# One encoder layer on one core: new orders of loads and output tiles, and weight sums made by accumulating loads instead of by GpSimd

## The chip, the cores and the metric

The kernel runs on one core of a Trainium2 chip: a tensor engine (TensorE, PE, with PEld loading its weights), a vector engine (VectorE, DVE), a scalar engine (ScalarE, ACT), GpSimd (POOL) and SyncE (SP), which only issues DMAs here. The metric is device time in microseconds (us) of one launch. Three runs of the kernel before took 1179.47, 1179.75 and 1180.17 us, median 1179.75.

## The reference

One layer of a streaming encoder on 1024 tokens of width 1024, in float32:

```
hn = rmsnorm(h)                       z = hn @ w_in
u, q, k, v = split(z)
h += concat(pool_mixer(u), chunk_attention(q, k, v)) @ w_out
hn = rmsnorm(h)                       up = hn @ w_up           # 1024 x 5632
gt, val = up[..., :2816], up[..., 2816:]
h += (gelu(causal_dwconv(gt)) * val) @ w_down
hn = rmsnorm(h)
h += sigmoid(hn @ w_ple_gate + b) * (p @ w_ple)
out = rmsnorm(h)
```

## The kernel before

Activations lie transposed, features on the partitions and tokens along the free axis, in two halves of 512 tokens (`HS[0]`, `HS[1]`). Every float32 product is three matmuls of split operands, `mm3` (lines 118 to 120: high by high, high by low, low by high). `split` makes the two parts: ACT copies the high part (line 123), DVE subtracts to get the low one (line 124).

**Start.** x arrives as 16 loads `x[k, h]`; beside them come parts of `w_qk0` (buffer `wq`) and of `w_v`. ACT makes the high part of the scaled x (line 215), DVE the low part (line 216), both are split parts of matmul operands. After each k, `start_mm(k)` adds the k-th terms: 12 matmuls 512 wide for q and k, and 9 matmuls 256 wide for the first three tiles of V.

**Attention, output projection.** Attention and pooling follow, then the output projection `out_mm` for the first half of the tokens and then, one output tile of 128 features after another, for the second. Around the second half the operands of the next stage ("forms") are made with `put`, a `split` into form n at place j.

**Up-projection.** Each of the 22 feature tiles `fi` holds gate and value columns. A 2 x 2 block product of weights (quarters 11, 12, 21, 22: gate or value by the first or second half of the input features) and activations (`b11, b12, b21, b22`) is done with seven products instead of eight, in the order 1, 5, 2, 6, 3, 7, 4, each 12 matmuls 512 wide. Products 1, 2 and 4 take a quarter of `w_up` as it is; 5, 6, 3 and 7 take sums or differences of quarters. A list `order` holds all products; `prepare` runs three ahead of the product being computed: it issues loads (`fetch`, SP), forms the sum (`summed`, line 687, a POOL operation on 128 x 512) in one of five raw buffers `rawu`, and splits it into one of three weight buffers `wu`. So the split for a product can start when the product three places earlier has left its buffer. Scheduling is by program order on each engine, with `high_priority` moving these splits and `keep` ahead of other work.

`step` takes what a product leaves in PSUM: `keep` (line 765) copies a result to SBUF on ACT; its copies of product 1 (`np1`) and 5 are used later; `u2` (line 781) is DVE's sum of product 6 with `np1`; lines 783 to 793 combine the rest; `gate` (802 to 805) is convolution and GELU; `values_in` (808, 809) multiplies the branches. Even tiles have 16 down-projection tiles of the pair of tiles before them placed after products 6, 3, 7 and 4; odd tiles have none, nor do tiles 0, 1, 20 and 21. Tile 0's products 1, 2, 5 and tile 1's product 1 come ahead of the rest, so that tile 0 goes on with 6, 3, 7, 4 after 5.

The last down-projections, the embedding gate and the final norm end the kernel.

Of the kernel before, what the change touches and what calls it, by code (L numbers as in the profile page):

```python
# [83 lines left out]
def trunk(tc, xT, pT, vecs, w_qk0, w_in, w_v, bias, counts, pool_w, w_out, w_up, w_down,  # L84
# [4 lines left out]
    with tc.tile_pool(name="sb", bufs=1) as sb, \  # L89
# [32 lines left out]
        def split(src, hi, lo):  # L122
            act.activation(hi, src, AF.Copy)  # L123
            dve.tensor_tensor(lo, src, rv(hi), ALU.subtract)  # L124
# [62 lines left out]
            return PS[:, (4, 5, 6, 4, 5, 6, 7, 3)[t], 0:256]  # L187

        def start_mm(k):
            for c in range(2):  # L190
                for h in range(2):
                    mm3(PS[:, 2 * c + h], w0h[:, k, c * P:(c + 1) * P], w0l[:, k, c * P:(c + 1) * P],
                        XTH[h][:, k], XTL[h][:, k], k == 0, k == KT - 1)
            for t in range(VT0):
                v_mm(t, k, v_ps(t), wv1)

# [6 lines left out]
        for k in range(KT):  # L203
            xs = xraw[k]
            for h in range(2):
                sp.dma_start(xs[:, h * 512:(h + 1) * 512], xT[k, :, h * 512:(h + 1) * 512])
                if k == 0 and h == 0:
                    act.dma_start(vec, vecs)
                if k in (0, 1, 4) and h == 0:
                    ke = (1, 4, 0, 0, 8)[k]  # L210
                    sp.dma_start(wq[:, k:ke], w_qk0[:, k * 256:ke * 256].rearrange("p (k c) -> p k c", c=256))
            g = vec[:, C_GMIX + k:C_GMIX + k + 1]
            for h in range(2):
                xk = xs[:, h * 512:(h + 1) * 512]
                act.activation(XTH[h][:, k], xk, AF.Copy, scale=g)
                dve.scalar_tensor_tensor(XTL[h][:, k], xk, g, rv(XTH[h][:, k]), ALU.mult, ALU.subtract)  # L216
                if h == 0:
                    split(wq[:, k], w0h[:, k], w0l[:, k])
            if k % 2 == 0:
                wv = wvraw[k // 2]  # L220
                sp.dma_start(wv, w_v[0, :, k * 256:(k + 2) * 256])
                wv = wv.rearrange("p (k c) -> p k c", k=2)
                split(wv, wv1[0][:, k:k + 2], wv1[1][:, k:k + 2])
# [10 lines left out]
        start_mm(KT - 1)  # L234

        def v_out(t, half, ps):
            s = rstd_tok[:, t:t + 1]
# [404 lines left out]
        def form_at(kb):  # L642
            a = r(kb, 4096).rearrange("p (x k t) -> p x k t", x=2, k=4)
            return a[:, 0], a[:, 1]

        forms = {1: form_at(64), 2: form_at(48), 3: form_at(16), 4: form_at(80), 5: form_at(0),
                 6: form_at(96), 7: form_at(112)}

        def put(n, j, src):
            split(src, forms[n][0][:, j], forms[n][1][:, j])  # L650


        wu = [r(32 + 4 * s, 1024).rearrange("p (x k c) -> p x k c", x=2, k=4) for s in range(3)]
# [1 line left out]
        rawd = f(42, 512)  # L655
        rst = f(44, SEQ)
        ahead = [(0, 1), (1, 1), (0, 2), (0, 5)]
        alone = ahead[:3]
        steps = {0: (6, 3, 7, 4), 1: (5, 2, 6, 3, 7, 4)}
        for fi in range(2, NF):  # L660
            steps[fi] = (1, 5, 2, 6, 3, 7, 4)
        order = ahead + [(fi, n) for fi in range(NF) for n in steps[fi]]

        loads = []
        for i, (fi, n) in enumerate(order):
            if (fi, n) in alone:
                loads += [(i, (fi, n), q) for q in FORMS[n]]
            else:
                need = {1: ((0, 0),), 5: ((1, 0), (1, 1)), 2: ((0, 1),), 6: ((0, 0),), 3: ((0, 1),), 7: (), 4: ()}[n]
                loads += [(i, fi, q) for q in need if not any(l[1] == fi and l[2] == q for l in loads)]  # L670
        prepared, fetched, done = [0], [0], [0]
        held = {}
        used = [False] * len(rawu)

        def fetch(upto):

            while fetched[0] < len(loads) and loads[fetched[0]][0] < upto and not used[fetched[0] % len(rawu)]:
                _, owner, (v, z) = loads[fetched[0]]
                i = fetched[0] % len(rawu)
                fetched[0] += 1  # L680
                used[i] = True
                fi = owner if isinstance(owner, int) else owner[0]
                sp.dma_start(rawu[i], w_up[fi, v, :, z * 512:(z + 1) * 512])
                held[owner, (v, z)] = i

        def summed(to, a, b, op=ALU.add):
            pool.tensor_tensor(rawu[to], rawu[a], rawu[b], op)  # L687
# [1 line left out]
        def prepare(upto):  # L689
            while prepared[0] < min(upto, len(order)):  # L690
                fi, n = order[prepared[0]]
                w_ = wu[prepared[0] % 3]
                prepared[0] += 1
                fetch(prepared[0] + 2)
                assert fetched[0] == len(loads) or loads[fetched[0]][0] >= prepared[0]
                if (fi, n) in alone:
                    t, = done_with = [held[(fi, n), q] for q in FORMS[n]]
                else:
                    a11, a12, a21, a22 = [held.get((fi, q)) for q in ((0, 0), (0, 1), (1, 0), (1, 1))]
                    if n == 5:  # L700
                        summed(a21, a21, a22)
                    elif n == 6:
                        summed(a21, a21, a11)
                    elif n == 3:
                        summed(a11, a21, a12)
                    elif n == 7:
                        summed(a21, a21, a22, ALU.subtract)
                    t = {1: a11, 5: a21, 2: a12, 6: a21, 3: a11, 7: a21, 4: a22}[n]
                    done_with = {3: [a11, a12], 7: [a21], 4: [a22]}.get(n, [])
                with tc.high_priority(AHEAD):  # L710
                    split(rawu[t].rearrange("p (k c) -> p k c", k=4), w_[:, 0], w_[:, 1])
                for q in done_with:
                    used[q] = False

        def product(bank, first):

            i = done[0]
            prepare(i + 1)
            fh, fl = forms[order[i][1]]
            w_ = wu[i % 3]  # L720
            for k in range(4):
                mm3(PS[:, bank], w_[:, 0, k], w_[:, 1, k], fh[:, k], fl[:, k], first and k == 0, k == 3, not first)
            done[0] += 1
            prepare(i + 4)

# [7 lines left out]
            weighted(0, d)  # L733
        for k in range(4):
            put(1, k, b11[k])
        for d in range(KT):
            out_mm(d, 1, d % 6, range(8), True, True)
            dve.tensor_tensor(H[d][:, HS[1]], H[d][:, HS[1]], PS[:, d % 6], ALU.add)
            norm_b.add(d)
            weighted(1, d)  # L740
            if d == 0:
                norm_a.sums()
            if d == 1:
                norm_a.rows(rst[:, HS[0]])
            if d < 4:
                pool.tensor_tensor(part[d % 2], b11[d], b12[d], ALU.subtract)
                put(5, d, part[d % 2])
# [76 lines left out]
        for n, src in ((7, b12), (4, b21)):  # L824
            for k in range(4):
                put(n, k, src[k])
# [4 lines left out]
        wd = [(B[:, 4096:5120], B[:, 5120:6144]), (B[:, 6144:7168], r(44, 1024))]  # L831

        def down_weights(fi, dst, raws=(rawd,)):
            for z in range(2):
# [63 lines left out]
        wg = [r(b, 2048) for b in (48, 56, 96, 104, 16, 24, 80, 88)]  # L898
        hp = [[(r(b, 512), r(b + 2, 512)) for b in bs]
              for bs in ((112, 116, 120, 124, 32, 36, 40, 44), (0, 4, 8, 12, 64, 68, 72, 76))]  # L900
        rawg = [f(44, 1024), f(48, 1024), f(52.25, 1024)]
        ng = [0]

# [168 lines left out]
```

## Time and profile before

| | |
|---|---|
| median of three runs | 1179.75 us (1179.47 to 1180.17) |
| the profiled execution's own time | 1180.88 us |
| its span, first to last instruction | 1179.1 us |
| granted TensorE clock, mean | 0.996 |
| instructions | 15388 |
| DMA | 70.79 MB in 34777 packets, mean 60 GB/s |

The profile's first part gives each engine's busy time with its share of the span in brackets and the number of its instructions after an x. In a group, "line engine operation out<-in xcount" is followed by the busy time, the mean of one in ns and the idle time ahead of it with what ended most of that. A row of the timeline begins with start and duration in us; a bracket at its end is the idle time ahead of it and what released it. A row of the waits names who waited, for whom, us in total, how often, and the longest. A row of windows gives the busy time of PE, PEld, DVE, ACT and POOL with counts, then the granted clock, the DMA share and GB/s. A row of the DMA issues gives the tensor, the queue, the count, the size of one and the median time from issue to landing.

### The profile page before, as it was taken

How to read it: one execution, taken by the hardware profiler on the slowest of the kernel's cores; microseconds unless marked ns; L12 is line 12 of the kernel's file. 1: busy time of each engine (PE TensorE's matmuls, PEld its weight loads, DVE VectorE, ACT ScalarE, POOL GpSimd, SP SyncE). 2: the span in 40 equal slices, each digit the busy share in tenths (PEclk: the TensorE clock that was granted, in tenths of full speed). 3: DMA queues.
4: the chain of work that ended last, by engine and by line, in shares of the span. 5: the costliest groups of instructions: out<-in, count | busy, mean ns of one | idle time of the engine just before them, and what ended most of it. 6: DMA issues, size and time to landing. Idle time of an engine off the chain costs nothing.

```text
span 1179.1 us, 15388 instructions
## 1 busy us (share of the span) xinstructions
PE 1159.2 (98%) x5829; PEld 979.5 (83%) x5829; DVE 876.2 (74%) x1405; ACT 542.1 (46%) x932; POOL 217.9 (18%) x194
## 2 busy tenths in 40 slices
PE   9999999999999989999999999999999999999996
PEld 7988998888888778888888888888888887888896
DVE  7678877879457887868777777777777779894454
ACT  7568686765555433324242424142424244554333
POOL 0000000181012431212121212121212123141000
PEclk9999999999999999999999999999999999999998
DMA  7110101106300120202020212111112121500021
GB/s 257 37 48 30 48 14 64 48 20 196 116 27 1 57 87 27 81 28 80 24 75 28 72 37 70 38 63 45 63 37 71 36 71 46 185 29 1 12 73 60
DMA packets 34777, 70.79 MB, mean 60 GB/s; under 512 B 3984, under 2 KB 6288, under 8 KB 34704
## 3 DMA queue, kind: packets, MB, share of 16 engines
q1 hardware_dynamic: 34560, 69.75, 18.2%
q8 instruction: 45, 0.74, 0.3%
q14 instruction: 28, 0.23, 0.1%
q10 hardware_dynamic: 144, 0.07, 0.0%
HBM read 65.61 MB, written 4.19 MB: 59 GB/s over the span
## 4 chain that ended last, share of the span: by engine, by line
PE 59%; issue 3%; DVE 2%; DMA 1%; POOL 1%; ACT 0%; DVEq 0%; POOLq 0%; ACTq 0%
PE PS L119 20%; PE PS L118 20%; PE PS L120 20%; DVE R L124 1%; POOL F L687 1%; DMA F<-in_w_down 1%; DMA F<-in_w_up 0%; DVE V L788 0%; DVE F L809 0%; PE PS L602 0%; ACT R L123 0%; DVE F L793 0%; PE PS L610 0%; DVE F L781 0%; DVE V L808 0%
## 5 line engine op out<-in xcount | busy, mean ns | idle before, releaser
L118 PE MATMUL PS<-R 128*128 128x512 f32 (+1 forms) x1144 | 430.0, 376 | 7.0 <-DVE F L781 3.2
L120 PE MATMUL PS<-R 128*128 128x512 f32 (+1 forms) x1144 | 426.7, 373 | 0.0
L119 PE MATMUL PS<-R 128*128 128x512 f32 (+1 forms) x1080 | 408.4, 378 | 0.3 <-DVE R L216 0.3
L118 PEld LDWEIGHTS PS<-R 128*128 128x128 f32 x1144 | 215.5, 188 | 45.0 <-ACT F L765 2.3
L120 PEld LDWEIGHTS PS<-R 128*128 128x128 f32 x1144 | 215.6, 188 | 38.2 <-DVE R L124 0.2
L123 ACT ACTIVATE R<-F 128x512 fp32r<-128x512 f32 (+2 forms) x217 | 135.3, 638 | 217.7 <-PE PS L119 173.0
L119 PEld LDWEIGHTS PS<-R 128*128 128x128 f32 x1080 | 203.6, 188 | 36.9 <-DVE R L216 0.9
L687 POOL TENSOR_TENSOR F<-F 128x512 f32<-128x512 f32 x88 | 139.4, 1584 | 512.2 <-DVE R L124 374.0
L124 DVE TENSOR_TENSOR R<-F,R 128x512 fp32r<-128x512 f32 (+2 forms) x213 | 161.1, 764 | 22.0 <-ACT R L123 19.3
L119 PE MATMUL PS<-B 128*128 128x512 f32 (+1 forms) x376 | 144.8, 385 | 0.0
L118 PE MATMUL PS<-B 128*128 128x512 f32 (+1 forms) x376 | 144.2, 383 | 0.0
L847 DVE TENSOR_TENSOR F<-F,PS 128x512 f32<-128x512 f32 x160 | 107.3, 683 | 21.6 <-PE PS L120 21.4
L123 ACT ACTIVATE B<-F 128x512 fp32r<-128x512 f32 (+1 forms) x83 | 58.0, 722 | 110.4 <-PE PS L119 74.4
L118 PEld LDWEIGHTS PS<-B 128*128 128x128 f32 x376 | 70.7, 188 | 15.0
L119 PEld LDWEIGHTS PS<-B 128*128 128x128 f32 x376 | 70.6, 188 | 14.3
L120 PE MATMUL PS<-B,R 128*128 128x512 f32 (+1 forms) x224 | 81.1, 362 | 0.0
L120 PE MATMUL PS<-B 128*128 128x512 f32 (+1 forms) x216 | 81.0, 375 | 0.0
L124 DVE TENSOR_TENSOR B<-F,B 128x512 fp32r<-128x512 f32 (+1 forms) x63 | 51.3, 841 | 9.6 <-ACT B L123 9.4
L338 ACT ACTIVATE F<-F,small 128x640 f32<-128x640 f32 (+2 forms) x64 | 44.4, 694 | 21.2 <-DVE small L336 13.0
L594 ACT ACTIVATE F<-F 128x512 f32<-128x512 f32 (+1 forms) x49 | 27.9, 570 | 51.2 <-DVE F L972 24.3
L360 DVE TENSOR_TENSOR B<-PS,B 128x640 fp32r<-128x640 f32 (+2 forms) x64 | 42.0, 656 | 9.2 <-ACT B L359 8.2
L120 PEld LDWEIGHTS PS<-B 128*128 128x128 f32 x216 | 40.5, 188 | 8.3
(145 smaller groups left out, 1560.2 us busy)
## 6 DMA issues: line engine op xcount, KB each, us to landing
F<-in_w_up SPq DMA_DIRECT2D x91, 256.0 KB, 2.6
F<-in_w_down SPq DMA_DIRECT2D x44, 256.0 KB, 2.6
F<-in_w_in SPq DMA_DIRECT2D x10, 512.0 KB, 3.5
F<-in_xT SPq DMA_DIRECT2D x16, 256.0 KB, 6.1
F<-in_w_out SPq DMA_DIRECT2D x16, 256.0 KB, 2.8
F<-in_xT SPq DMA_DIRECT2D x8, 512.0 KB, 3.6
F<-in_w_gate SPq DMA_DIRECT2D x8, 512.0 KB, 3.5
F<-in_bias SPq DMA_DIRECT2D x8, 320.0 KB, 2.9
```

The source lines that it names most:

```text
L118: pe.matmul(ps, ahi, bhi, start=first, stop=False, skip_group_check=more)
L119: pe.matmul(ps, ahi, blo, start=False, stop=False, skip_group_check=more)
L120: pe.matmul(ps, alo, bhi, start=False, stop=last, skip_group_check=more)
L123: act.activation(hi, src, AF.Copy)
L124: dve.tensor_tensor(lo, src, rv(hi), ALU.subtract)
L338: act.activation(S[:, 0:n], S[:, 0:n], AF.Exp, bias=s_[:, 0:1], scale=-1.0, accum_out=s_[:, 1:2])
L360: dve.tensor_tensor(lo, pst, rv(hi), ALU.subtract)
L594: act.activation(self.q, src, AF.Square)
L687: pool.tensor_tensor(rawu[to], rawu[a], rawu[b], op)
L847: dve.tensor_tensor(H[d][:, HS[h]], H[d][:, HS[h]], PS[:, bank], ALU.add)
```

## The change

Four parts, in one edit.

1. *Sums by accumulating loads.* For tiles in `by_load`, here all 22, `fetch` loads the first quarter of a chain with SP and issues the others as accumulating DMAs from POOL's queue into the same buffer. Product 5's buffer later grows into 6 (after the split for 5) and 3 (after the split for 6) by two further accumulating loads issued in `prepare`; 7's is a buffer of its own. Each tile then takes five loads on SP and four accumulating ones on POOL. `fetch` runs one place earlier for these tiles.

```
+        by_load = range(NF)
+        chains = {1: ((0, 0),), 5: ((1, 0), (1, 1)), 2: ((0, 1),), 7: ((1, 0), (0, 0)), 4: ((1, 1),)}
+        grows = {5: (0, 0), 6: (0, 1)}
...
+                if place >= upto + (fi in by_load):
+                    break
...
+                sp.dma_start(rawu[i], quarter(fi, qs[0]))
+                for q in qs[1:]:
+                    pool.dma_start(rawu[i], quarter(fi, q), accum_op=ALU.add)
...
-                if (fi, n) in alone:
-                    t, = done_with = [held[(fi, n), q] for q in FORMS[n]]
+                if fi in by_load:
+                    m = n if n in chains else 5
+                    t = held[(fi, m), chains[m][0]]
+                    done_with = [] if n in grows else [t]
...
                     split(rawu[t].rearrange("p (k c) -> p k c", k=4), w_[:, 0], w_[:, 1])
+                if fi in by_load and n in grows:
+                    pool.dma_start(rawu[t], quarter(fi, grows[n]), accum_op=ALU.add)
```

2. *Start.* The matmuls of `start_mm` run half by half, the V matmuls of step k run after the q and k matmuls of step k+1 (`start_v(k - 1)`), `w_v` is loaded in odd steps, and the parts of `w_qk0` at other places.

```
-                if k in (0, 1, 4) and h == 0:
-                    ke = (1, 4, 0, 0, 8)[k]
+                if (k, h) in ((0, 0), (0, 1), (3, 1)):
+                    ka, ke = {(0, 0): (0, 1), (0, 1): (1, 4), (3, 1): (4, 8)}[k, h]
...
+                if k % 2 and h == 0:
+                    sp.dma_start(wvraw[k // 2], w_v[0, :, (k - 1) * 256:(k + 1) * 256])
...
             if k < KT - 1:
                 start_mm(k)
+            if k:
+                start_v(k - 1)
```

3. *Output tiles of the second half* in the order 0, 4, 1, 5, 2, 6, 3, 7; the puts of forms 6 and 7 are made among them, those of form 2 and POOL's subtractions on b21 are spread. Forms lie at other addresses.

```
-        for d in range(KT):
-            out_mm(d, 1, d % 6, range(8), True, True)
+        for z, d in enumerate((0, 4, 1, 5, 2, 6, 3, 7)):
+            k = z // 2
+            out_mm(d, 1, z % 6, range(8), True, True)
...
-                k = d - 4
-                put(2, k, b21[k])
                 dve.tensor_tensor(b12[k], b12[k], b22[k], ALU.subtract)
                 dve.tensor_tensor(b11[k], b11[k], b12[k], ALU.subtract)
-                pool.tensor_tensor(b21[k], b21[k], b11[k], ALU.subtract)
-            if d == 5:
+                put(6, k, b11[k])
+                put(7, k, b12[k])
+            for j in {2: (0,), 4: (1, 2), 6: (3,)}.get(z, ()):
+                put(2, j, b21[j])
+            for j in {2: (0,), 4: (1,), 5: (2,), 7: (3,)}.get(z, ()):
+                pool.tensor_tensor(b21[j], b21[j], b11[j], ALU.subtract)
+            if z == 5:
                 prepare(3)
...
-        for k in range(4):
-            put(6, k, b11[k])
         step(0, 2)
```

4. *Last tile.* The `w_down` tiles of the last two feature tiles are loaded and split one after product 3, one after product 4, instead of both after 3.

```
-                             3: lambda: [down_weights(fi, wd2[fi % 2], raw_last[fi % 2]) for fi in last_f]})
+                             3: lambda: down_weights(last_f[0], wd2[0], raw_last[0]),
+                             4: lambda: down_weights(last_f[1], wd2[1], raw_last[1])})
```

How instructions stand on an engine, at three places. A row is line, operation, output<-input, size, and the semaphores waited for; PE, Activation, DVE and Pool are those of engines, DMAHW those of loads issued by SP, DMASW those of loads issued by POOL.

ACT at the start, from the first x tile on, before. Line 215 makes the high part of x, line 224 is the square, the row into `B` is the split of `w_v`:

```order
L215 ACTIVATE R<-F,vec 128x512 [waits DMAHW1_49,DMAHW0_49]
L123 ACTIVATE R<-F 128x256 [waits DMAHW2_49]
L215 ACTIVATE R<-F,vec 128x512 [waits DMAHW3_49]
L123 ACTIVATE B<-F 128x512 [waits DMAHW4_49]
L224 ACTIVATE F<-F 128x1024 [waits DVE_49]
L215 ACTIVATE R<-F,vec 128x512 [waits DMAHW5_49]
L123 ACTIVATE R<-F 128x256 [waits DMAHW6_49]
L123 ACTIVATE R<-F 128x256
L215 ACTIVATE R<-F,vec 128x512 [waits DMAHW7_49]
```

The same place after the change, where line 219 is x and line 226 the square:

```order
L219 ACTIVATE R<-F,vec 128x512 [waits DMAHW1_49,DMAHW0_49]
L123 ACTIVATE R<-F 128x256 [waits DMAHW2_49]
L219 ACTIVATE R<-F,vec 128x512 [waits DMAHW3_49]
L123 ACTIVATE R<-F 128x256 [waits DMAHW4_49]
L226 ACTIVATE F<-F 128x1024 [waits DVE_49]
L219 ACTIVATE R<-F,vec 128x512 [waits DMAHW5_49]
L123 ACTIVATE B<-F 128x512 [waits DMAHW6_49]
L219 ACTIVATE R<-F,vec 128x512 [waits DMAHW7_49]
L123 ACTIVATE R<-F 128x256
```

The split of `w_v` moved behind the second x tile, and a split of `w_qk0` stands ahead of the square.

ACT in an even tile, from the split for product 5 on, before. Line 805 is GELU, line 765 the copy of product 1 (`np1`); the splits that wait for Pool are those for 5, 6 and 3:

```order
L123 ACTIVATE R<-F 128x512 [waits PE_49,Activation_49,Pool_49]
L123 ACTIVATE R<-F 128x512 [waits DMAHW6_49,PE_49,Activation_49]
L805 ACTIVATE F<-F 128x1024 [waits DVE_49]
L123 ACTIVATE R<-F 128x512 [waits PE_49,Pool_49]
L765 ACTIVATE F<-PS 128x512 [waits PE_49]
L123 ACTIVATE R<-F 128x512 [waits PE_49,Activation_49,Pool_49]
```

After the change, GELU is line 827 and the copy is line 787, the splits for 5 and 6 wait for DMASW:

```order
L123 ACTIVATE R<-F 128x512 [waits DMASW0_49,PE_49,Activation_49]
L123 ACTIVATE R<-F 128x512 [waits DMAHW1_49,PE_49,Activation_49]
L827 ACTIVATE F<-F 128x1024 [waits DVE_49]
L123 ACTIVATE R<-F 128x512 [waits DMASW2_49,PE_49,Activation_49]
L787 ACTIVATE F<-PS 128x512 [waits PE_49]
L123 ACTIVATE B_3423<-F 128x512 [waits DVE_49,Activation_49]
L787 ACTIVATE V<-PS 128x512 [waits PE_49]
L123 ACTIVATE B_3423<-F 128x512 [waits DVE_49]
```

The split ahead of the copy of `np1` now waits for an accumulating load instead of a POOL operation, and a split for the down-projection (into `B`) stands between the two copies, where that for product 3 stood.

DVE in the last tile, from the value product (line 809) to u2 (line 781), before; 793 is `gate0`:

```order
L809 TENSOR_TENSOR F<-F,V 128x1024 [waits DVE_49]
L124 TENSOR_TENSOR R<-F,R 128x512 [waits PE_49,Activation_49]
L124 TENSOR_TENSOR R<-F,R 128x512 [waits DMAHW7_49]
L124 TENSOR_TENSOR R<-F,R 128x512 [waits DMAHW5_49]
L124 TENSOR_TENSOR R<-F,R 128x1024 [waits DVE_49,Activation_49]
L124 TENSOR_TENSOR R<-F,R 128x512 [waits PE_49,Activation_49]
L793 TENSOR_TENSOR F<-PS,F 128x512
L124 TENSOR_TENSOR R<-F,R 128x512 [waits DMAHW4_49,Activation_49]
L124 TENSOR_TENSOR R<-F,R 128x512 [waits DMAHW3_49]
L781 TENSOR_TENSOR F<-PS,F 128x512 [waits PE_49]
```

After the change, with u2 on line 803, `gate0` on 815 and the value product on 831:

```order
L831 TENSOR_TENSOR F<-F,V 128x1024 [waits DVE_49]
L124 TENSOR_TENSOR R<-F,R 128x512 [waits DMAHW5_49,PE_49,Activation_49]
L124 TENSOR_TENSOR R<-F,R 128x512 [waits DMAHW6_49,Activation_49]
L124 TENSOR_TENSOR R<-F,R 128x1024 [waits DVE_49,Activation_49]
L124 TENSOR_TENSOR R<-F,R 128x512 [waits DMASW7_49,PE_49,Activation_49]
L124 TENSOR_TENSOR R<-F,R 128x512 [waits DMASW5_49,PE_49,Activation_49]
L815 TENSOR_TENSOR F<-PS,F 128x512
L803 TENSOR_TENSOR F<-PS,F 128x512 [waits PE_49]
```

Two subtractions of the `w_down` splits fewer stand ahead of u2, and the two weight splits ahead of `gate0` wait for accumulating loads.

More of the change, by code (lines that the diff above doesn't have):

```diff
@@ L189, in start_mm, with start_v @@
         def start_mm(k):
-            for c in range(2):
-                for h in range(2):
+            for h in range(2):
+                for c in range(2):
                     mm3(PS[:, 2 * c + h], w0h[:, k, c * P:(c + 1) * P], w0l[:, k, c * P:(c + 1) * P],
                         XTH[h][:, k], XTL[h][:, k], k == 0, k == KT - 1)
+        def start_v(k):
             for t in range(VT0):
@@ L218, in trunk @@
                     split(wq[:, k], w0h[:, k], w0l[:, k])
[L219 to L223, printed above, removed]
+            if k % 2:
+                wv = wvraw[k // 2].rearrange("p (k c) -> p k c", k=2)
+                split(wv, wv1[0][:, k - 1:k + 1], wv1[1][:, k - 1:k + 1])
             act.activation(xs, xs, AF.Square)
@@ L234, in trunk @@
         start_mm(KT - 1)
+        start_v(KT - 1)
         def v_out(t, half, ps):
@@ L640, in trunk @@
                for n in (range(2, 10), (10, 11, 12, 13, 14, 15, 0, 1))[h]] for h in range(2)]
[L642 to L647, printed above, removed]
+        form_kb = {1: (64, 68, 72, 76), 2: (44, 48, 52, 56), 3: (16, 20, 24, 28), 4: (80, 84, 88, 92),
+                   5: (0, 4, 8, 12), 6: (96, 104, 112, 120), 7: (100, 108, 116, 124)}
+        forms = {n: [(r(kb, 512), r(kb + 2, 512)) for kb in kbs] for n, kbs in form_kb.items()}
         def put(n, j, src):
-            split(src, forms[n][0][:, j], forms[n][1][:, j])
+            split(src, *forms[n][j])
         wu = [r(32 + 4 * s, 1024).rearrange("p (x k c) -> p x k c", x=2, k=4) for s in range(3)]
@@ L657, in trunk @@
         ahead = [(0, 1), (1, 1), (0, 2), (0, 5)]
-        alone = ahead[:3]
         steps = {0: (6, 3, 7, 4), 1: (5, 2, 6, 3, 7, 4)}
@@ L662, in trunk @@
         order = ahead + [(fi, n) for fi in range(NF) for n in steps[fi]]
+        by_load = range(NF)
+        chains = {1: ((0, 0),), 5: ((1, 0), (1, 1)), 2: ((0, 1),), 7: ((1, 0), (0, 0)), 4: ((1, 1),)}
+        grows = {5: (0, 0), 6: (0, 1)}
         loads = []
         for i, (fi, n) in enumerate(order):
-            if (fi, n) in alone:
-                loads += [(i, (fi, n), q) for q in FORMS[n]]
+            if fi in by_load:
+                if n in chains:
+                    loads.append((i, (fi, n), chains[n]))
             else:
                 need = {1: ((0, 0),), 5: ((1, 0), (1, 1)), 2: ((0, 1),), 6: ((0, 0),), 3: ((0, 1),), 7: (), 4: ()}[n]
-                loads += [(i, fi, q) for q in need if not any(l[1] == fi and l[2] == q for l in loads)]
+                loads += [(i, fi, (q,)) for q in need if not any(l[1:] == (fi, (q,)) for l in loads)]
         prepared, fetched, done = [0], [0], [0]
@@ L675, in fetch @@
         def fetch(upto):
-            while fetched[0] < len(loads) and loads[fetched[0]][0] < upto and not used[fetched[0] % len(rawu)]:
-                _, owner, (v, z) = loads[fetched[0]]
+            while fetched[0] < len(loads) and not used[fetched[0] % len(rawu)]:
+                place, owner, qs = loads[fetched[0]]
+                fi = owner if isinstance(owner, int) else owner[0]
+                if place >= upto + (fi in by_load):
+                    break
                 i = fetched[0] % len(rawu)
@@ L681, in fetch, with quarter @@
                 used[i] = True
-                fi = owner if isinstance(owner, int) else owner[0]
-                sp.dma_start(rawu[i], w_up[fi, v, :, z * 512:(z + 1) * 512])
-                held[owner, (v, z)] = i
+                sp.dma_start(rawu[i], quarter(fi, qs[0]))
+                for q in qs[1:]:
+                    pool.dma_start(rawu[i], quarter(fi, q), accum_op=ALU.add)
+                held[owner, qs[0]] = i
+        def quarter(fi, q):
+            return w_up[fi, q[0], :, q[1] * 512:(q[1] + 1) * 512]
         def summed(to, a, b, op=ALU.add):
@@ L695, in prepare @@
                 assert fetched[0] == len(loads) or loads[fetched[0]][0] >= prepared[0]
-                if (fi, n) in alone:
-                    t, = done_with = [held[(fi, n), q] for q in FORMS[n]]
+                if fi in by_load:
+                    m = n if n in chains else 5
+                    t = held[(fi, m), chains[m][0]]
+                    done_with = [] if n in grows else [t]
                 else:
@@ L718, in product @@
             prepare(i + 1)
-            fh, fl = forms[order[i][1]]
+            form = forms[order[i][1]]
             w_ = wu[i % 3]
             for k in range(4):
-                mm3(PS[:, bank], w_[:, 0, k], w_[:, 1, k], fh[:, k], fl[:, k], first and k == 0, k == 3, not first)
+                mm3(PS[:, bank], w_[:, 0, k], w_[:, 1, k], *form[k], first and k == 0, k == 3, not first)
             done[0] += 1
@@ L823, in trunk @@
         norm_b.rows(rst[:, HS[1]])
-        for n, src in ((7, b12), (4, b21)):
-            for k in range(4):
-                put(n, k, src[k])
+        for k in range(4):
+            put(4, k, b21[k])
         t_pool.__exit__(None, None, None)
@@ L830, in trunk @@
         gv = [B[:, 2048 * s:2048 * (s + 1)] for s in range(2)]
-        wd = [(B[:, 4096:5120], B[:, 5120:6144]), (B[:, 6144:7168], r(44, 1024))]
+        wd = [(B[:, 4096:5120], B[:, 5120:6144]), (B[:, 6144:7168], r(60, 1024))]
         def down_weights(fi, dst, raws=(rawd,)):
```

16 lines of the change are left out of this document (8 added, 8 removed).

## The prediction

> **What bounds the kernel now.** I read the page first, then TensorE's busy time in windows, then the waits of TensorE, and last the timeline around each wait.
>
> ```profile
> PE 1159.2 (98%) x5829; PEld 979.5 (83%) x5829; DVE 876.2 (74%) x1405; ACT 542.1 (46%) x932; POOL 217.9 (18%) x194
> 480.00:520.00 40.00, 40.00 (x176) 32.80 (x175) 31.46 (x42) 12.84 (x18) 9.76 (x6) 1.00 0.10 34
> ```
>
> The second row is 40 us of the up-projection: TensorE is busy all of it at a granted clock of 1.00, 176 matmuls, so one starts every 40/176 = 0.227 us and a product of 12 lasts 2.73 us. The change removes no matmul. POOL's 9.76 us and a DMA share of 0.10 are cover, not bound. Time can only come from the few places where TensorE stops; of its waits these three concern the change:
>
> ```profile
> PE PS L118 <- DVE F L781: 3.2, 2, 1.7
> PE PS L118 <- ACT F L765: 1.9, 1, 1.9
> PE PS L118 <- ACT V L765: 0.9, 1, 0.9
> ...
> 394.64 0.50 PE L118 MATMUL PS<-R 128*128 128x512 f32 x1 [0.86 <-ACT V L765]
> 415.47 0.47 PE L118 MATMUL PS<-R 128*128 128x512 f32 x1 [1.43 <-DVE F L781]
> 428.53 0.50 PE L118 MATMUL PS<-R 128*128 128x512 f32 x1 [1.92 <-ACT F L765]
> 1001.14 0.47 PE L118 MATMUL PS<-R 128*128 128x512 f32 x1 [1.73 <-DVE F L781]
> ```
>
> Call the four stops A, B, C, D: 0.9 + 1.4 + 1.9 + 1.7 = 5.9 us, all at the entry to the up-projection or just after its last tile. That is the most the change can give there. Everywhere else in the 22 tiles a sum has hidden cover, and the question is whether what replaces it has cover too.
>
> **The price of an accumulating load.** The change drops 88 sums on POOL and issues 88 accumulating loads from POOL's queue; w_up transfers go from 91 to 198 (110 on SP, 88 on POOL).
>
> ```profile
> L687 POOL TENSOR_TENSOR F<-F 128x512 f32<-128x512 f32 x88 | 139.4, 1584 | 512.2 <-DVE R L124 374.0
> F<-in_w_up SPq DMA_DIRECT2D x91, 256.0 KB, 2.6
> F<-in_w_in SPq DMA_DIRECT2D x10, 512.0 KB, 3.5
> F<-in_xT SPq DMA_DIRECT2D x16, 256.0 KB, 6.1
> 394.34 0.33 SPq L836 DMA_DIRECT2D F<-in_w_down  x1
> ```
>
> This trace has no accumulating load and no DMA of POOL's at all. Let L be the time from POOL being released to the sum standing in the buffer. Low bound: a plain load of the same 256 KB, 2.6. High bound: the same load while eight queue at the start, 6.1. I take 4.1: 2.6, plus 0.9 for 256 KB more on the way (3.5 - 2.6; the destination is read as well as written), plus 0.6 for POOL's part of the issue, the middle between nothing and what one POOL pass over the tile takes beyond SP's issue (1.58 - 0.33 = 1.25). It is nearest to the 512 KB row, since 16 engines at a share of 0.10 are not the crowd of the 6.1 row. The 107 additional transfers of 256 KB are 28 MB over some 620 us, 45 GB/s on top of 34: a cost of nothing while the share stays near 0.2.
>
> The Trainium skill, "DMA: Bandwidth & Descriptors", section "Anatomy of one DMA — SWDGE (gpsimd) path", gives a load issued by GpSimd 2.0 us plus bytes over 436 GB/s, an estimate of 2.6 for one without addition; by it L would sit at my low bound and the sum below would be 0.5 lower. No run so far shows it.
>
> An addition cannot start before the buffer's split is done (wake 0.1, an estimate), and a split after it takes 0.63 on ACT, then DVE 0.69: 1.3.
>
> **A, entry to tile 0 (saves 0.6).** ACT's copy `keep` stands behind puts that wait for POOL's subtractions on b21, queued behind POOL's sums. Those sums go and the puts are spread. New: tile 0 runs 5, 6, 3 consecutively, so two additions are in series into one buffer.
>
> ```profile
> 382.40 0.69 DVE L124 TENSOR_TENSOR R<-F,R 128x512 fp32r<-128x512 f32 x1
> ```
>
> Split 5 ends at 383.1; two rounds of 0.1 + L + 1.3 end at 385.9 + 2L = 394.1 for L = 4.1. TensorE could go on at 394.64 - 0.86 = 393.8. Left over 0.3, saved 0.6; 2 us for each us of L.
>
> **B (saves 1.4).** DVE is behind by 1.4 us when u2 (L781) is due. Operations beside a POOL sum were stretched:
>
> ```profile
> 398.19 1.78 DVE L124 TENSOR_TENSOR R<-F,R 128x512 fp32r<-128x512 f32 x1
> 403.09 2.29 DVE L803 SCALAR_TENSOR_TENSOR F<-F,vec 128x1024 f32<-128x1024 f32 x1 [0.72 <-ACT F L802]
> ...
> 542.06 1.28 DVE L803 SCALAR_TENSOR_TENSOR F<-F,vec 128x1024 f32<-128x1024 f32 x1
> ```
>
> L124 takes 1.78 against 0.69, L803 2.29 against 1.28 away from POOL: 2.1 us back from these two alone, and the puts of forms 6 and 7 leave this stretch for the output projection. Both exceed 1.4. What is next there is another POOL-free operation, so I give all 1.4.
>
> **C (saves 1.9).** The copy of np1 stood on ACT behind the split of a w_down load, with a second split between:
>
> ```profile
> 426.85 0.63 ACT L123 ACTIVATE B<-F 128x512 fp32r<-128x512 f32 x1 [0.41 <-DMA F<-in_w_down]
> 427.90 0.58 ACT L765 ACTIVATE F<-PS 128x512 f32<-128x512 f32 x1
> ```
>
> The new order on ACT puts split 6 and `keep` ahead of the w_down split. If split 6 is on time, the stop goes: 1.9.
>
> **D, last tiles (saves 1.5).** u2 stood behind seven splits on DVE, five of them in the last row but one below; two of the seven, of a w_down tile, move one product later.
>
> ```profile
> 965.87 0.69 DVE L124 TENSOR_TENSOR R<-F,R 128x512 fp32r<-128x512 f32 x1
> 977.47 0.39 PE L118 MATMUL PS<-R 128*128 128x512 f32 x1
> 984.94 0.69 DVE L124 TENSOR_TENSOR R<-F,R 128x512 fp32r<-128x512 f32 x1
> 996.53 0.39 PE L118 MATMUL PS<-R 128*128 128x512 f32 x1
> 994.58 4.02 DVE L124 TENSOR_TENSOR R<-F,R 128x512 fp32r<-128x512 f32 x5 [0.62 <-ACT R L123]
> 1000.32 0.68 DVE L781 TENSOR_TENSOR F<-PS,F 128x512 f32<-128x512 f32 x1
> ```
>
> Two splits fewer are 2 x 0.69 = 1.4 and their waits, so the 1.7 goes. But tiles 20 and 21 have no down-projection between products: from split 5 (ends 966.6 and 985.6) two rounds end at 969.4 + 2L and 988.4 + 2L, and product 3 is due at 977.5 and 996.5. Both need L up to 4.05; at 4.1 they are late by 0.1 each. Saved 1.7 - 0.2 = 1.5, slope 4 for each us of L.
>
> **Steady tiles (0).** Ten even tiles, 2 to 20. Their rows:
>
> ```profile
> 543.25 0.69 DVE L124 TENSOR_TENSOR R<-F,R 128x512 fp32r<-128x512 f32 x1
> 544.02 3.99 POOL L687 TENSOR_TENSOR F<-F 128x512 f32<-128x512 f32 x2 [5.35 <-DVE R L124]
> 546.73 0.63 ACT L123 ACTIVATE R<-F 128x512 fp32r<-128x512 f32 x1 [0.49 <-PE PS L119]
> 547.27 0.58 ACT L765 ACTIVATE F<-PS 128x512 f32<-128x512 f32 x1
> 549.42 0.39 PE L118 MATMUL PS<-R 128*128 128x512 f32 x1
> ```
>
> Split 5 ends at 543.94. ACT's split 6 now waits for the addition and stands ahead of the copy of np1, which product 2 (549.42) needs. So 543.94 + 0.1 + L + 0.63 + 0.58 must not pass 549.42: L up to 4.2. At 4.1 it fits by 0.1 us; beyond 4.2 it costs 10 us for each us of L. Odd tiles:
>
> ```profile
> 528.35 0.69 DVE L124 TENSOR_TENSOR R<-F,R 128x512 fp32r<-128x512 f32 x1 [0.73 <-ACT R L123]
> 535.82 0.39 PE L118 MATMUL PS<-R 128*128 128x512 f32 x1
> ```
>
> Split 6 ends at 529.04 and product 3 starts at 535.82: 529.04 + 0.1 + L + 1.3 fits for L up to 5.4, another 10 us for each us beyond. POOL's queue is in order: the additions for 5 and 7 are ahead of those for 6 and 3 and wait only for loads, issued a product earlier than before. Behind a late one stands the next POOL addition and no one else.
>
> **Start (+0.8).** V matmuls move a step later, w_v loads move behind x, and ACT no longer splits w_v before the first square.
>
> ```profile
> 4.00:8.00 4.00, 2.89 (x8) 1.53 (x7) 2.09 (x5) 1.74 (x3) 0.00 (x0) 1.00 0.82 213
> 8.00:12.00 4.00, 3.77 (x11) 3.00 (x12) 1.51 (x3) 2.87 (x6) 0.00 (x0) 0.57 1.04 399
> 12.00:16.00 4.00, 4.00 (x25) 3.49 (x24) 4.00 (x8) 4.00 (x7) 0.00 (x0) 1.00 0.97 346
> 7.44 0.50 PE L118 MATMUL PS<-R 128*128 128x512 f32 x1 [1.06 <-ACT R L215]
> 12.70 0.74 DVE L216 SCALAR_TENSOR_TENSOR R<-F,vec,R 128x512 fp32r<-128x512 f32 x1
> ```
>
> By data both orders are tied to the x tile whose low half L216 finishes at 13.4: TensorE holds the same matmuls by then. But without V matmuls in the first step it can run dry at 10.5 to 11.4, and here a gap of 1.06 us was followed by four microseconds at 0.57 of the clock. A second such window loses 4 x 0.43 = 1.7. I take half, 0.8 (bounds: -1, the gap of 1.06 filled; +1.7).
>
> The Trainium skill, "TensorE: Matmul & The Clock Gate", section "Why this matters for your kernels", asks only that TensorE not idle over about 3 us; by it no window is lost and the sum is 0.8 lower. The trace disagrees so far: 0.57 after a gap of 1.06.
>
> **Sum.** -0.6 - 1.4 - 1.9 - 1.5 + 0.8 = -4.6 us. The profiled execution took 1180.88 us, so 1176.3; the median shown, 1179.75, is 1.1 below that execution, so the forecast is **1175.2 us**. For other L the change is -4.6 + 6(L - 4.1), with 10(L - 4.2) added above 4.2: -2.4 at 4.3, 0 at 4.45, +8.8 at 5.0, +12 at 5.2.
>
> **The rivals.**
>
> *The copy of np1 comes late in every even tile (slower).* For: 0.1 us of slack, on an L that no row shows, and ACT's order puts `keep` behind the addition. Against: low bound 2.6 leaves 1.6 of slack. It decides from L = 4.45; with L = 5.0 the time is 1179.75 + 8.8 = 1188.6, and with 5.2 1191.8.
>
> *POOL is held up by DVE while it issues (slower).* For: POOL and DVE stretch each other in this trace:
>
> ```profile
> 546.77 1.78 DVE L788 TENSOR_TENSOR V<-V 128x512 f32<-128x512 f32 x1
> ```
>
> One DVE operation of 1.28 to 1.78 ahead of each issue makes L 5.4 to 5.9: +15 to +28 (by the formula, and at the upper end 5 more for the odd tiles), 1195 to 1208. Against: that stretch was with POOL reading whole tiles. The Trainium skill, "SBUF — State Buffer", section "Summary: rules for kernel authors", says that GpSimd's descriptor writing is starved while VectorE is in its fast two-port modes, and advises another queue; no row here shows it.
>
> *Gains and losses cancel (same).* L of 4.35 (-1.6 by the formula), and a whole second slow window at the start (+0.9 more): 1179.1.
>
> *Even better.* L of 2.6 removes what is left of A and D and no window is lost: -5.9 us, 1173.9; with the start's gain of 1, 1172.8.
>
> **How the numbers follow.** Forecast 0.36, even better 0.12: faster 0.48. Same 0.15. Late copy 0.28 and held-up POOL 0.09: slower 0.37. About 0.2% (2.4 us) is what a measurement of this kernel can tell from no change. The range runs from the best case, 1172.5, to the late copy at L = 5.2, 1192; above it lie the held-up POOL and the tail of the late copy, some 0.15. The faster cases alone would give 1172.5 to 1177.3.
>
> **What would show it.** The DMA issues give L directly: 4.2 or less, and the ten even tiles show no TensorE idle ahead of product 2; above, each shows L - 4.2 released by ACT's copy. The three wait rows quoted above are gone but for 0.3 at A; DVE's 1.78 rows are gone with POOL's sums; 8:12 and 12:16 show whether a window is lost. The prediction is wrong if L exceeds 4.45, if stops A to D stay although L is short, or if a wait appears at a place not named here, such as product 7 or 3 of odd tiles.

## The result and the profile after

The changed kernel took 1191.04 us (median of six runs, 1189.39 to 1195.8) against 1179.95 for the kernel before (1179.47 to 1181.38): ratio 1.0098, 95% interval [1.0088, 1.0109]. It is slower by 11 us, where 4.6 less was forecast. The profiled execution took 1190.8 us.

The page, TensorE's waits and the DMA issues of the changed kernel. The last two rows are of `w_up`: queue, count, size, median from issue to landing.

```profile
PE 1163.2 (98%) x5829; PEld 978.7 (82%) x5829; DVE 838.9 (71%) x1405; ACT 541.2 (46%) x932; POOL 155.7 (13%) x194
...
L124 DVE TENSOR_TENSOR R<-F,R 128x512 fp32r<-128x512 f32 (+2 forms) x213 | 147.9, 701 | 92.4 <-ACT R L123 89.8
...
PE PS L118 <- ACT F L787: 7.5, 10, 2.9
PE PS L615 <- POOL small L611: 3.1, 2, 2.1
...
PE PS L118 <- ACT V L787: 2.3, 1, 2.3
...
F<-in_w_up SPq DMA_DIRECT2D x110, 256.0 KB, 2.8
F<-in_w_up POOLq DMA_DIRECT2D x88, 256.0 KB, 4.3
```

VectorE is relieved by 37 us (876.2 to 838.9) and u2 is waited for no more: line 803 is not in the list. In its place stand ten waits for ScalarE's copy of product 1 (line 787 into `F`), one of 2.3 us for that of product 5 (into `V`), and a longer one at the end for line 611. TensorE has 5829 matmuls in both kernels, and from the up-projection on they stand in the same order. There the start of one and the same matmul in the two traces tells how far the changed kernel is behind at that place (first matmul after each stop):

| place | before | after | behind by |
|---|---|---|---|
| A, product 3 of tile 0 | 394.64 | 394.75 | 0.1 |
| product 7 of tile 0 | 397.50 | 399.13 | 1.6 |
| B, product 7 of tile 1, after its u2 | 415.47 | 415.47 | 0.0 |
| C, product 2 of tile 2 | 428.53 | 428.00 | -0.5 |
| product 2 of tile 20 | 972.03 | 977.45 | 5.4 |
| product 2 of tile 21 | 991.10 | 999.76 | 8.7 |
| D, after u2 of tile 21 | 1001.14 | 1008.37 | 7.2 |
| transpose of the norm | 1062.45 | 1071.86 | 9.4 |
| last matmul | 1171.41 | 1180.99 | 9.6 |

Up to A it is ahead by 1.3 us. It loses 1.4 at A and 1.5 just behind it, gains 1.6 at B and 0.5 at C, loses 5.9 over tiles 4 to 20, 1.8 at tiles 20 and 21 with D in it, and 2.2 at the end.

An even tile, 10, in the order of time: the timeline of ScalarE, VectorE, POOL and TensorE of the changed kernel.

```profile
664.80 0.63 ACT L123 ACTIVATE R<-F 128x512 fp32r<-128x512 f32 x1 [1.06 <-DMA F<-in_w_up]
665.47 0.69 DVE L124 TENSOR_TENSOR R<-F,R 128x512 fp32r<-128x512 f32 x1 [0.30 <-ACT R L123]
666.56 0.88 POOL L729 DMA_DIRECT2D F<-in_w_up  x1 [3.97 <-DVE R L124]
670.74 0.63 ACT L123 ACTIVATE R<-F 128x512 fp32r<-128x512 f32 x1 [2.29 <-DMA F<-in_w_up]
671.27 0.58 ACT L787 ACTIVATE F<-PS 128x512 f32<-128x512 f32 x1
671.90 0.50 PE L118 MATMUL PS<-R 128*128 128x512 f32 x1 [0.51 <-ACT F L787]
```

Read it backwards. TensorE stood 0.51 us until the copy of np1 was done; the copy stood behind the split for 6; that waited 2.29 us for the accumulating load; POOL issued it at 666.56, 0.40 after VectorE's part of split 5 ended (666.16); and split 5 itself had waited 1.06 us for its own accumulating load. Two loads in series, each with an addition, now lie ahead of a copy that never depended on them.

How long the loads take, by line: 729 issues those for 6 and 3, 694 those for 5 and 7, in us from issue to landing (least, median, most).

```profile
L729 POOL DMA_DIRECT2D F<-in_w_up x44: 858/875/927, 382.5 to 1000.4; - x44
...
DMA to landing us min/median/max: 3.9/4.0/4.7
...
L694 POOL DMA_DIRECT2D F<-in_w_up x44: 860/867/1113, 298.5 to 987.9; - x44
...
DMA to landing us min/median/max: 3.7/4.7/6.6
```

The loads of line 729 run alone, or beside the tail of one of line 694. Those of line 694 come in pairs, mostly 1 to 2 us apart, and there one takes up to 6.6.

The entry to tile 0, product 2 of tile 2 (C), tile 21 and the end:

```profile
393.06 1.15 ACT L123 ACTIVATE R<-F 128x512 fp32r<-128x512 f32 x2 [5.33 <-DMA F<-in_w_up]
394.12 0.58 ACT L787 ACTIVATE V<-PS 128x512 f32<-128x512 f32 x1
...
394.75 0.79 PE L118 MATMUL PS<-R 128*128 128x512 f32 x1 [2.26 <-ACT V L787]
...
396.00:400.00 4.00, 4.00 (x14) 3.17 (x14) 2.30 (x5) 0.85 (x2) 0.86 (x1) 0.75 0.54 160
...
428.00 0.50 PE L118 MATMUL PS<-R 128*128 128x512 f32 x1 [1.37 <-ACT F L787]
...
SPq L692 <- DMA F<-in_w_up: 8.0, 1, 8.0
...
982.72 0.69 DVE L124 TENSOR_TENSOR R<-F,R 128x512 fp32r<-128x512 f32 x1 [1.41 <-ACT R L123]
...
983.44 2.73 SPq L692 DMA_DIRECT2D F<-in_w_up  x3
986.53 0.86 POOL L694 DMA_DIRECT2D F<-in_w_up  x1 [7.61 <-DMA F<-in_w_up]
992.69 1.16 ACT L123 ACTIVATE R<-F 128x512 fp32r<-128x512 f32 x2 [3.45 <-DMA F<-in_w_up]
999.76 0.50 PE L118 MATMUL PS<-R 128*128 128x512 f32 x1 [2.86 <-ACT F L787]
...
SPq L855 <- DMA F<-in_w_up: 16.8, 1, 16.8
```

At A it is the copy of product 5 that stands behind the split for 3, whose load is the second in series in one buffer; the stop grew from 0.86 to 2.26 us, and the clock granted to the 14 matmuls of the window after it was 0.75. At tile 21 the first quarter for 5 goes into the buffer in which the sums of tile 20 grew. SyncE waited 8.0 us for the last load into it and then for VectorE's part of the split for 3 (ended at 983.41), and issued at 983.44; POOL's load, issued at 986.53, held ScalarE until 992.69. It is so in every tile from 1 on: the first quarter for 5 is issued 0.02 to 0.03 us after the split for 3 of the tile before. At the end SyncE's queue stood 16.8 us for a `w_up` buffer before it could issue a `w_down` load.

### The profile page after: what moved, and what is told of

Same layout as the page of the kernel before. It is cut to its first block, busy times and chain, and to the rows that moved or that the text cites. A ratio compares the mean times of both kernels' runs of the same rounds, so it can differ in the third digit from the quotient of the medians.

```text
span 1189.0 us, 15476 instructions
## 1 busy us (share of the span) xinstructions
PE 1163.2 (98%) x5829; PEld 978.7 (82%) x5829; DVE 838.9 (71%) x1405; ACT 541.2 (46%) x932; POOL 155.7 (13%) x194
## 5 line engine op out<-in xcount | busy, mean ns | idle before, releaser
L124 DVE TENSOR_TENSOR R<-F,R 128x512 fp32r<-128x512 f32 (+2 forms) x213 | 147.9, 701 | 92.4 <-ACT R L123 89.8
L729 POOL DMA_DIRECT2D F<-in_w_up x44 | 38.5, 875 | 372.1 <-DVE R L124 372.1
L118 PEld LDWEIGHTS PS<-B 128*128 128x128 f32 x376 | 70.7, 188 | 15.0
L119 PEld LDWEIGHTS PS<-B 128*128 128x128 f32 x376 | 70.6, 188 | 14.3
L694 POOL DMA_DIRECT2D F<-in_w_up x44 | 38.6, 882 | 214.7 <-DVE F L866 73.0
L124 DVE TENSOR_TENSOR B<-F,B 128x512 fp32r<-128x512 f32 (+1 forms) x63 | 52.1, 842 | 9.2 <-ACT B L123 9.0
```

Source lines behind the costliest of these rows:

```text
L118: pe.matmul(ps, ahi, bhi, start=first, stop=False, skip_group_check=more)
L119: pe.matmul(ps, ahi, blo, start=False, stop=False, skip_group_check=more)
L694: pool.dma_start(rawu[i], quarter(fi, q), accum_op=ALU.add)
L729: pool.dma_start(rawu[t], quarter(fi, grows[n]), accum_op=ALU.add)
```

## The experiments

All ratios are to runs of the kernel before on the same chip in the same job.

**1. Copies on VectorE.**

```
-                act.activation(dst, PS[:, bank], AF.Copy, scale=scale)
+                dve.tensor_scalar(dst, PS[:, bank], scale, 0.0, ALU.mult, ALU.add)
```

> The changed kernel with the copies of products 1 and 5 made by VectorE instead of ScalarE, so that no copy stands behind a split that waits for an accumulating load. Theory 1 (the loss in the even tiles is the place of the copy on ScalarE): the ten waits for the copy, 7.5 us, and most of the 2.3 us at the entry to tile 0 go; 1182 us, between 1180 and 1184. Theory 2 (the accumulating loads are too slow whatever stands behind them): TensorE waits as long, now for the splits of products 6 and 3; 1189 to 1192 us.

Measured 1190.86 us (1187.93 to 1191.07), ratio 1.0078 [1.0058, 1.0098]: the total hardly moved, which looks like theory 2. TensorE's waits say otherwise:

```profile
PE PS L118 <- ACT R L123: 4.1, 3, 2.0
PE PS L615 <- POOL small L611: 3.3, 2, 2.3
PE PS L119 <- DVE B L124: 2.6, 1, 2.6
```

The ten waits for the copies are gone. From 550 to 977 us of the changed kernel's trace this one gains 4.9 us on it, matmul by matmul, but a new wait of 2.6 us for a `w_down` split on VectorE, in tile 2, up to 436.33, and two windows at half clock (from 436.24 and 1071.12, 3.41 us each) took that back. That split stood on VectorE behind a weight split that waited 1.73 us for ScalarE. Whether the copy of product 5 or those of tiles 0 to 2 on VectorE brought this on was not tested apart; experiment 6 moves neither, and has no such wait.

**2. Loads in tiles 0 and 1 alone.**

```
-        by_load = range(NF)
+        by_load = (0, 1)
```

> The changed kernel with accumulating loads in tiles 0 and 1 alone; the other 20 tiles are summed by GpSimd again. If the loss of the steady tiles (6.0 us over tiles 4 to 20) and the excess at tile 21 over before (1.8 us) come from accumulating loads: 1191.0 - 7.8 = 1183 us, and less by up to 2.2 if the late end follows from tile 21's stop. If additional DMA traffic or the other orders cost the time: above 1187 us.

1179.61 us (1177.55 to 1181.67), ratio 0.9987 [0.9977, 0.9997]. The whole loss is in the accumulating loads of the other 20 tiles, the end included: its wait for line 611 is 1.0 us, as before, with the later `w_down` load in place.

```profile
PE PS L118 <- DVE F L803: 2.0, 1, 2.0
...
PE PS L615 <- POOL small L611: 1.0, 1, 1.0
```

The wait for u2 of tile 21 (line 803) is there again although the later `w_down` load is in place; the stop at C is gone.

**3. Last tile as before.**

```
-                             3: lambda: down_weights(last_f[0], wd2[0], raw_last[0]),
-                             4: lambda: down_weights(last_f[1], wd2[1], raw_last[1])})
+                             3: lambda: [down_weights(fi, wd2[fi % 2], raw_last[fi % 2]) for fi in last_f]})
```

> The changed kernel with both w_down tiles of the last two feature tiles loaded and split after product 3 again. Theory 3 (the later w_down load holds SyncE's queue, so the w_gate loads behind it come late and the norm at the end waits 2.2 us): the wait there goes, two more splits stand ahead of u2 for up to 1.4 us; 1189 to 1190 us. Rival (the end is late because tile 21 stops TensorE): 1191 us or more, the wait stays.

1194.49 us (1192.23 to 1197.34), ratio 1.0115 [1.0091, 1.014]; the wait stayed.

```profile
PE PS L615 <- POOL small L611: 3.5, 2, 2.5
...
SPq L855 <- DMA F<-in_w_up: 14.0, 1, 14.0
```

Theory 3 falls: where `down_weights` is called does not decide it. SyncE waits as before for a buffer of `w_up`. That gave theory 4, below. TensorE does not wait for u2 of tile 21 here either, with both `w_down` tiles after product 3. The profile has two windows at half clock, from 980.66 and 1072.82, where the changed kernel has one.

**4. The new start alone**, put into the kernel before (the diff is part 2 of the change).

> The kernel before with the new start alone (orders of the loads and matmuls of the first 35 us). By the shift of the matmuls in the two traces up to the entry to tile 0: 1.3 us less, 1178.6 us. If the gain is given back in the attention, where other engines set the pace: 1180 us. As forecast, with half a slow window: 1180.8 us.

1180.91 us (1179.3 to 1183.91), ratio 1.0004 [0.9993, 1.0015]: nothing. In its profile the matmuls lead those of before by 1.5 us, as they did up to A in the changed kernel; but the profiled execution of before had a window at half clock there (8:12 at 0.57 in the forecast's rows) and this one had none, and over all runs the two kernels are alike, their fastest at 1179.3 and 1179.4.

**5. Another raw buffer for the last `w_down` tile.**

```
-        raw_last = [(rawu[nl % 5], rawd), (rawu[(nl - 4) % 5], rawu[(nl - 1) % 5])]
+        raw_last = [(rawu[nl % 5], rawd), (rawu[(nl - 3) % 5], rawu[(nl - 1) % 5])]
```

> The changed kernel with one raw buffer of the last w_down tile exchanged: that of product 2 of the last tile instead of that of its products 5, 6 and 3, which is free only when the split for product 3 is done. Theory 4 (SyncE waits 16.8 us for that buffer, and the w_down and w_gate loads behind it, their splits on ScalarE and VectorE and the norm at the end come late): the wait for line 611 at the end falls from 3.1 to about 1.0 us, 1189 us. Rival (tile 21's stop delays the end): the wait stays, 1191 us.

1195.4 us (1191.42 to 1198.35), ratio 1.0126 [1.0107, 1.0146]. In TensorE's waits the end does what theory 4 says, and the rest does not:

```profile
PE PS L118 <- ACT F L787: 9.9, 10, 2.3
...
PE PS L118 <- ACT R L219: 2.2, 1, 2.2
...
PE PS L615 <- POOL small L611: 1.0, 1, 1.0
```

The wait for line 611 fell from 3.1 to 1.0, and between tile 21 and the norm this kernel gains 2.3 us on the changed one. In the same profile it had lost 2.6 us on it up to A and 4.7 from 550 to 977 us, places that the edit does not touch, with windows at half clock from 12.69, 398.39 and 985.49. So the cause of the late end is shown, its worth in the total is not; why this kernel met more slow windows stays open.

**6. The copy of product 1 alone on VectorE, from tile 3 on.**

```
             if n == 1 and fi != 1:
-                keep(np1, x, -1.0)
+                if fi > 2:
+                    with tc.high_priority(AHEAD):
+                        dve.tensor_scalar(np1, PS[:, x], -1.0, 0.0, ALU.mult, ALU.add)
+                else:
+                    keep(np1, x, -1.0)
```

> The changed kernel with the copy of product 1 alone made by VectorE from tile 3 on; the copies of product 5 and those of tiles 0 to 2 stay on ScalarE. Theory 1: the shift over tiles 4 to 20, 6.0 us in the changed kernel, goes, and the 2.9 us of tile 21 in part: 1183 to 1185 us. Theory 2: TensorE waits as long for the splits of product 6: 1190 us.

1184.96 us (1184.9 to 1188.34), ratio 1.0049 [1.0034, 1.0065]: 6.1 us below the changed kernel. Its timeline in an even tile:

```profile
667.34 0.68 DVE L796 TENSOR_SCALAR F<-PS 128x512 f32<-128x512 f32 x1
...
668.78 0.63 ACT L123 ACTIVATE R<-F 128x512 fp32r<-128x512 f32 x1 [2.19 <-DMA F<-in_w_up]
669.45 0.69 DVE L124 TENSOR_TENSOR R<-F,R 128x512 fp32r<-128x512 f32 x1 [1.43 <-ACT R L123]
```

Split 6 waits for its load as long as ever, 2.19 us, but the copy is done at 668.02 without it, and TensorE has no wait at all between 440 and 970 us, where the changed kernel has seven for line 787. Theory 1 holds: the load was not too late for the product that uses it, only for the copy queued behind it.

**7. Own buffers for the sums of tile 0**, with loads in tiles 0 and 1 alone.

```
+        own = {6: ((1, 0), (1, 1), (0, 0)), 3: ((1, 0), (1, 1), (0, 0), (0, 1))}
...
-                if n in chains:
-                    loads.append((i, (fi, n), chains[n]))
+                c = {**chains, **own} if fi == 0 else chains
+                if n in c:
+                    loads.append((i, (fi, n), c[n]))
```

> Accumulating loads in tiles 0 and 1 alone, and in tile 0 the sums for products 6 and 3 have buffers and loads of their own (five more transfers of 256 KB), so that they need not wait for the splits for 5 and 6. Theory 5 (the stop at the entry to tile 0, 2.7 us and the slow clock behind it 1.7 us, comes from two accumulating loads in series in one buffer): both go, 1179.6 - 3.5 = 1176 us. Rival (the copy there waits for something else, or the additional loads delay the queue of GpSimd): 1179 us or more.

1176.15 us (1175.47 to 1177.82), ratio 0.9967 [0.9954, 0.9979]: 0.3% faster than the kernel before. Of its waits only D is left in the up-projection, and the window after tile 0's entry is at full clock:

```profile
PE PS L118 <- DVE F L806: 1.7, 1, 1.7
...
392.00:396.00 4.00, 4.00 (x20) 3.30 (x19) 2.61 (x5) 1.79 (x3) 0.87 (x1) 1.00 0.45 95
```

**8. Loads in the odd tiles, and 9. in the even tiles.**

```
+        by_load = (0, 1, *range(3, NF - 2, 2))     # 8
+        by_load = (0, 1, *range(2, NF - 2, 2))     # 9, with the edit of 7
```

> Accumulating loads in tiles 0 and 1 and in the nine odd tiles 3 to 19; the even tiles from 2 on and tile 21 are summed by GpSimd. Theory 1 (only where the copy of product 1 stands behind an accumulating load and no down-projection gives room does it cost): as with loads in tiles 0 and 1 alone, 1179.6 us, within 1. Theory 2 (every tile of accumulating loads costs about 0.6 us): 1179.6 + 9 x 0.6 = 1185 us.

> The kernel with own chains in tile 0 and accumulating loads in tiles 0 and 1, with accumulating loads in the even tiles 2 to 18 added; copies stay on ScalarE. Theory 1 (the copy of product 1 behind the split that waits for the load): the waits for the copy come back, 1.5 us at tile 2 and 0.6 to 0.7 in each of eight tiles, 1176.2 + 6.7 = 1183 us. Rival (neither parity costs anything by itself; the loss needs loads in all tiles, by their traffic): 1176 to 1178 us.

Odd tiles: 1179.45 us (1178.64 to 1182.26), ratio 0.9996 [0.9987, 1.0005], within 0.2 us of experiment 2. Even tiles: 1184.57 us (1181.4 to 1186.91), ratio 1.0025 [1.0014, 1.0036], 8.4 above experiment 7, where 6.7 was expected; the two ran on different chips, and by their ratios to the kernel before the difference is 6.8. TensorE's waits in 9 between 440 and 970 us:

```profile
PE PS L118 <- ACT F L790: 4.7, 7, 1.3
```

In 8 that stretch has none. Accumulating loads in nine odd tiles cost nothing, in nine even ones 0.8 to 0.9 us a tile: it is the place, not the load.

**10. All 22 tiles with the edits of 5, 6 and 7.**

> Accumulating loads in all 22 tiles with the three mends together: product 1 copied by VectorE from tile 3 on, own chains in tile 0, the other raw buffer for the last w_down tile. If the causes add up: 1191.0 - 6.1 (copy) - 3.5 (tile 0) - 2.1 (end) = 1179.4 us, with what is left at tiles 20 and 21. If they do not, a wait takes their place: 1183 us or more.

1183.51 us (1181.86 to 1185.95), ratio 1.0021 [1.0011, 1.003]. The causes do not add up: 4.1 us of the forecast gain are missing. By the same comparison of matmuls, against experiment 7, it loses 1.9 us up to tile 4, 0.5 from there to tile 20, and 4.0 at tiles 20 and 21, in this profile with a window at half clock from 998.56. The waits there are for line 790 (the copy of product 5) and for a split:

```profile
PE PS L615 <- POOL small L611: 2.6, 2, 1.5
PE PS L118 <- ACT V L790: 1.9, 1, 1.9
...
PE PS L118 <- ACT R L123: 1.4, 1, 1.4
```

Tiles 20 and 21 have too little room for loads in series even so, and 1.9 us of a late end are back.

## Why the prediction was wrong

*What bounds the kernel.* Right: all that moved are stops of TensorE and the windows at half clock behind some of them, and the steady cover decided.

*The price of a load.* Right in size: 4.1 forecast, 4.0 measured from issue to landing for line 729; its three terms were not measured apart. The estimate "wake 0.1" was wrong: POOL started 0.40 after VectorE. That makes 4.5 to 4.8 from the end of split 5 to the start of split 6 in the even tiles, over the 4.3 (0.1 + 4.2) that the forecast's limit allowed. By the Trainium skill, "DMA: Bandwidth & Descriptors", section "Anatomy of one DMA — SWDGE (gpsimd) path", the estimate for a plain load is 2.6; the accumulating loads here took 4.0 alone and up to 6.6 in pairs, so its estimate does not hold for them.

*Steady tiles (0 forecast, 5.9 measured).* This is the step that failed. Its mechanism was named, as the first rival, and its limit was right to 0.1 us; it failed by two terms. One is the 0.3 us of POOL's start. The other is the sentence that the additions for 5 "wait only for loads, issued a product earlier": they do, but the first of these loads starts no earlier than the split for 3 of the tile before, which frees its buffer. In even tiles the addition comes with that for 7, takes 4.4 to 4.9 us, and split 5 waited 0.6 to 1.1 us for it; against product 5 it ended up to 0.43 us later than in the kernel before. The forecast summed one load where the path has two. Averaged over the nine even tiles 4 to 20, a tile costs 0.68 us: 0.29 by the longer path from split 5 to the copy, 0.24 by the later split 5, and 0.15 at the restart, where the first matmul takes 0.50 us instead of 0.39. The rival's price, 1188.6 us at L = 5.0, is near the result by luck: from split 5 to split 6 these tiles take 4.59 us on average, which in the forecast's sum (0.1 + L) is an L of 4.5, and for that its formula gives 1180.6.

*A (-0.6 forecast, +1.4 and 1.5 for a slow window measured).* Two loads in series were counted, but up to the split for 3, not to the copy of product 5 behind it on ScalarE, and the second took 4.7 us. In experiment 7 the sums for 6 and 3 have buffers of their own, no addition waits for a split of tile 0, and the stop is gone.

*B (-1.4 forecast, -1.6 measured).* Right: the stop is gone, and L124's mean fell from 764 to 701 ns without POOL's sums. Whether the sums or the moved puts of forms 6 and 7 did it was not tested apart.

*C (-1.9 forecast, -0.5 measured).* The `w_down` split left, and the split for 6 took its place: TensorE waited 1.37 us there for line 787. The condition of the forecast, split 6 on time, is what failed: with tile 2 summed by POOL (experiment 2) the stop is gone.

*D (-1.5 forecast, +1.8 measured, tile 21 included).* The wait for u2 went, as forecast, but not by the two splits moved behind u2: with them moved and tile 21 summed by POOL it stayed (2.0 us in experiment 2, 1.7 in 7), and in experiment 3, with accumulating loads and the splits not moved, it was gone. That part came right by luck, and what took the wait away stays open. And 2.86 us ahead of product 2 came instead. The forecast looked at product 3 and gave split 5 its old time; the first quarter for 5 had to wait for the buffer of tile 20's sums, and the addition was then 6.05 us on the way beside that for 7.

*The end (no term, +2.2 measured).* Not foreseen: a raw buffer that is released only after the last accumulating load was also the buffer of a `w_down` load, and SyncE's queue behind it holds the rest. Experiment 5 shows it at its place.

*Start (+0.8 forecast, 0 measured).* Experiment 4. The rule of the Trainium skill, "TensorE: Matmul & The Clock Gate", section "Why this matters for your kernels", that idle up to about 3 us loses no clock is not borne out: the slow window of 0.75 above followed a stop of 2.26.

*POOL held up by VectorE.* Not seen: POOL's part of an issue took 0.86 to 0.93 us in the steady tiles, once 1.11.

## What to carry to other kernels

When a wait is made longer, the instruction that waits need not be the one that pays: list what stands behind it on its in-order queue, and cost the path to each of those, from the first load in series on, and from the release of the buffer that it fills. A resource's release counts as well as its filling: a buffer that is let go later is somebody else's late load. And when an edit's total does not move, compare the same matmul in both traces place by place before giving up the theory; in experiment 1 a gain of 4.9 us was hidden under a new wait and two slow windows.

## What the runs showed of the hardware

TensorE's clock was halved for 3.41 us at a time, which costs up to 1.7 us (1.5 by the matmuls behind A), mostly as work resumed after a stop of about 2 us or more: after 2.26 at A in the changed kernel, 2.6 in experiment 1 up to 436.33, 2.2 at the start of experiment 5 (12:16 at 0.59). A stop of 2.86 at tile 21 of the changed kernel was not followed by one, nor one of 2.29 at A in experiment 3, and before had one after 1.06, so no threshold follows from these runs. Two accumulating loads of 256 KB issued 1.3 us apart at tile 21, with a plain load issued between them, took 6.05 and 6.06 us, one alone 4.0 (median of line 729); plain loads took 2.8. VectorE's operations that took 1.78 us beside POOL's sums took 0.69 beside POOL's DMA issues.
